# Global attention with its maxima in pairs of banks, its scores in single banks, its values two fifths at a time and the result's last two operations half a unit later

## The chip, the cores and the metric

One core of a Trainium2 chip runs the kernel. The metric is device time in microseconds (us) of one execution: 1538.0 us is the median of three (1535.93 to 1540.02). The engines are TensorE (PE, matrix products, with PEld for its weight loads), VectorE (DVE), ScalarE (ACT), GpSimd (POOL) and SyncE (SP), which issues the DMA transfers. "KB each" and shapes are those of the profile; everything is float32 unless a row says otherwise.

## The reference

Two layers (DEPTH) of a block over 1024 latent tokens and 256 context tokens, width 1024. One input projection feeds three groups of heads: A is global attention (8 heads of 64, 2 key heads, over all 1280 tokens), B a pooling mixer, C neighbourhood attention. Each result is multiplied by its own gate, all are joined and projected back:

```
aq, ak, av, ag, bz, bg, nq, nk, nv, ng = jnp.split(h @ w_in[l], SPLIT_POINTS, axis=-1)
...
def dense_attn(q, k, v):
    s = jnp.einsum("bqkgd,bskd->bkgqs", q, k).astype(jnp.float32)
    p = jax.nn.softmax(s, axis=-1).astype(v.dtype)
    o = jnp.einsum("bkgqs,bskd->bqkgd", p, v)
...
y = jnp.concatenate([a_out * silu(ag), b_out * silu(bg), n_out * silu(ng)], axis=-1) @ w_out[l]
x = x + gate[:, None] * y
```

## The kernel before, in words

Each layer runs in stages: the projections, the neighbourhood attention, the global attention, the output projection. The change is about the third stage and its seams with the second and fourth.

**The units of global attention.** There are 8 in a layer (`ga_unit`), each for 512 queries and a pair of heads of one key head. Scores are computed transposed: keys on the partitions, queries along the row. The 1280 keys are ten tiles of 128; two tiles make a fifth (`kp` 0 to 4). `scores(hi, kp)` does 4 matmuls for head `hi`, fifth `kp` (two tiles, each a product with `k1` and one with `k2`; the second also subtracts the softmax's shift, which lies in a row of `q2`) into a pair of banks, and ACT takes the exponential of all 1024 columns (L1032) into a tile `gp`. POOL adds the tiles of one head up (L1037 the first two, L1040 the next), DVE adds the last (L1040 too) and folds the halves (L1042). `values` multiplies a fifth with the value rows into the accumulator bank `ps_c`, one fifth behind the scores; the last copies the bank out (L1053, `gosb`).

**The maxima ("shifts").** The shift of the softmax is the exact row maximum, so the scores are computed once more with the queries on the partitions: per head 8 matmuls of 512 keys and 2 steps with 2 x 256 keys, each step in one single bank, each followed by a DVE reduction (L1004, L1009). These 20 steps of unit n, and a 21st that turns the result into a row (`shift_rows`, L1017, L1019, two small DMAs), are done ahead: a list `shifts` is worked off in between, 29 steps ahead of the scores. The first 29 are done in the last 10 units of the neighbourhood attention of layer 0 (the last 7 in layer 1), 3 per unit.

**The finish** of unit n comes within unit n+1, at `kp` 2: column sums (L1058, `ones` times the accumulators), a gate's DMA (L1060), logarithm and exponential for the reciprocal (ACT, L1062, L1063) with one correction step (DVE, L1065, L1066), gate times result (POOL, L1067), the product of both (DVE, L1068), and `store_u`, which splits it into a high part (ACT, L815) and a low part (DVE, L816). For the last unit it comes behind the first loads of the output projection's weights. Those are split the same way by `split_w` (ACT L287 high, DVE L288 low), three buffers `woraw`, one weight tile per k.

**What sets the order.** PE's instructions run in the order in which the code issues them (L97, `manual_schedule`). The orders of ACT, DVE, POOL and SP are made by the framework's scheduler; each engine then works its list strictly in order. PSUM has 8 banks: three single ones in rotation (`ps_b`, taken by `ps_one`), one accumulator (`ps_c`), and two pairs (`ps_w`, taken by `ps_pair`). The tiles `gp` and the accumulators `gacc` share a ring of seven buffers (tag "prob"); keys of both attentions share six buffers (`kst`).

**Neighbourhood attention** has 28 units in layer 0 (eight of them for the context's queries) and 16 in layer 1. `early(i, fn)` puts a load ahead of unit i: the queries of the first two global units at the twelfth unit from the end, the keys (`gk(0)`, three transfers) in both layers later. A unit waits on its own gate (L834), which goes through POOL (L869) before PE's transposes (L882).

Of the kernel before, what the change touches and what calls it, by code (L numbers as in the profile page):

```python
# [74 lines left out]
def hybrid_block_kernel(  # L75
# [298 lines left out]
    for l in range(DEPTH):  # L374
# [600 lines left out]
        def ga_unit(cc, g, pr):  # L975
# [16 lines left out]
            def shift(i):  # L992

                hi, j = divmod(i, 10)
                if i == 0:
# [4 lines left out]
                S = ps_one("ps_m")  # L1000
                if j < 8:
                    qt, half = divmod(j, 2)
                    PE.matmul(S, q1[:, qt * P:(qt + 1) * P], k1[:, half * 512:(half + 1) * 512], start=True, stop=True)  # L1003
                    DVE.reduce_max(out=mx[:, qt, half:half + 1], in_=S, axis=AX.X)  # L1004
                    return
                q0 = 2 * (j - 8)
                for i in range(2):
                    PE.matmul(S[:, i * 256:(i + 1) * 256], q1[:, (q0 + i) * P:(q0 + i + 1) * P], k1[:, SEQ:NT], start=True, stop=True)
                DVE.reduce_max(out=mx[:, q0:q0 + 2, 2], in_=S.rearrange("p (a b) -> p a b", a=2), axis=AX.X)  # L1009
                if hi and j == 9:  # L1010
                    st.nn = small.tile([P, 8], F32, tag="gnn", name="gnn")
                    DVE.tensor_reduce(out=st.nn, in_=st.mx.rearrange("p h q k -> p (h q) k"), op=ALU.max, axis=AX.X, negate=True)
# [11 lines left out]
            def scores(hi, kp):  # L1024
                k1, k2 = gk(g)
                S = ps_pair("ps_st").rearrange("p (a b) -> p a b", a=2)
                for i in range(2):
# [1 line left out]
                    PE.matmul(S[:, i, :], k1[:, kc], st.q1[hi], start=True, stop=False)  # L1029
                    PE.matmul(S[:, i, :], k2[:, kc], st.q2[hi], start=False, stop=True)  # L1030
# [1 line left out]
                ACT.activation(out=p, in_=S, func=AF.Exp)  # L1032
# [303 lines left out]
```

## Time and profile before

| | |
|---|---|
| median of three runs | 1538.0 us (1535.93 to 1540.02) |
| profiled execution | 1539.72 us, span 1537.9, clock 0.996 |
| busy PE, PEld, DVE, ACT, POOL | 1474.2, 1072.8, 860.2, 637.6, 513.1 us |
| a middle unit of global attention | 27.1 us, PE busy 25.85 |
| units 0, 6, 7 of layer 0 | 23.2, 26.7, 31.8 us |
| values, L1049 | x640, 165.0 us, mean 609 ns |
| maxima, L1004, DVE | x256, 171.7 us, mean 685 ns |
| exponentials, L1032, ACT | x160, 162.4 us, mean 1022 ns |
| adds, L1040, POOL | x64, 161.4 us, mean 2548 ns |

PE's row says "busy" from a matmul's start to its modelled end, and neighbours overlap; the distance of two starts shows what one really costs. In a row of waits stand the total, how often, and the longest; in a window's row its length, then busy time of PE, PEld, DVE, ACT and POOL, PE's clock, the share of the DMA engines and GB/s.

### The profile page before, as it was taken

To read this page: it belongs to the slowest core of one execution; us is meant where nothing else is said; L and a number is where in the kernel's file an instruction comes from. 1 tells how busy PE (TensorE), PEld (TensorE's weight loads), DVE (VectorE), ACT (ScalarE), POOL (GpSimd) and SP (SyncE) were. 2 spreads that over 40 slices of the span, in tenths; PEclk is the share of its full clock that TensorE was granted. 3 is DMA by queue.
4 is the path that set the end of the run, shared out by engine and by line. 5 is a ranking of instruction groups with operands and counts; after the bars stand their busy time and mean duration, and the time that the engine had idled before them with its cause. 6 is when DMAs were issued, how large, how long until landed. Compare 5 with 4: busy or idle time off the path is not lost.

```text
span 1537.9 us, 22259 instructions
## 1 busy us (share of the span) xinstructions
PE 1474.2 (96%) x8001; PEld 1072.8 (70%) x8001; DVE 860.2 (56%) x1666; ACT 637.6 (41%) x1220; POOL 513.1 (33%) x630
## 2 busy tenths in 40 slices
PE   5999999999999999998999999999998999999999
PEld 3787777788888555553788888878787854544577
DVE  3645234552678678875533543464358868786522
ACT  4543132333676444444312452332466544444400
POOL 0232336000134556565001233460013265565300
PEclk9999999999999999999999999999999999999999
DMA  9436455537745200101413222243697301001331
GB/s 317 140 97 219 133 158 162 165 107 192 178 113 159 73 27 25 39 8 55 168 58 109 76 93 91 85 142 82 155 227 172 89 21 42 21 24 39 133 121 55
DMA packets 153039, 167.91 MB, mean 109 GB/s; under 512 B 35384, under 2 KB 112032, under 8 KB 152864
## 3 DMA queue, kind: packets, MB, share of 16 engines
q1 hardware_dynamic: 152928, 166.48, 37.0%
q8 instruction: 63, 1.03, 0.3%
q14 instruction: 48, 0.39, 0.1%
HBM read 126.45 MB, written 40.86 MB: 109 GB/s over the span
## 4 chain that ended last, share of the span: by engine, by line
PE 80%; DVE 8%; ACT 4%; DMA 3%; issue 3%; SPq 1%; POOL 0%; DVEq 0%; POOLq 0%; ACTq 0%
PE ps_w L418 8%; PE ps_w L419 8%; PE ps_w L420 8%; PE ps_c L1049 8%; PE ps_w L1204 4%; PE ps_w L1207 4%; PE ps_w L1205 4%; PE ps_w L1029 4%; PE ps_b L1003 4%; PE ps_w L1030 3%; PE ps_c L894 3%; PE ps_b L882 2%; PE ps_w L426 2%; PE ps_w L428 2%; PE ps_w L427 2%
## 5 line engine op out<-in xcount | busy, mean ns | idle before, releaser
L1032 ACT ACTIVATE gp<-ps_w 128x1024 f32<-128x1024 f32 x160 | 162.4, 1022 | 190.9 <-PE ps_w L1030 155.3
L418 PE MATMUL ps_w<-wh,hh 128*128 128x512 f32 (+1 forms) x624 | 235.7, 378 | 2.2 <-ACT wh L287 2.2
L419 PE MATMUL ps_w<-wl,hh 128*128 128x512 f32 (+1 forms) x624 | 229.0, 367 | 1.0 <-DVE wl L288 1.0
L420 PE MATMUL ps_w<-wh,hl 128*128 128x512 f32 (+1 forms) x624 | 228.4, 366 | 0.0
L1004 DVE TENSOR_REDUCE gmx<-ps_b 128x1 f32<-128x512 f32 x256 | 171.7, 685 | 73.2 <-PE ps_b L1003 69.0
L1049 PE MATMUL ps_c<-gp,av 128*64 128x512 f32 x640 | 165.0, 609 | 10.3 <-ACT gp L1032 10.3
L1040 POOL TENSOR_TENSOR gacc<-gacc,gp 128x1024 f32<-128x1024 f32 x64 | 161.4, 2548 | 25.8 <-ACT gp L1032 25.5
L418 PEld LDWEIGHTS ps_w<-wh,hh 128*128 128x128 f32 x624 | 118.4, 190 | 27.8 <-issue 4.0
L419 PEld LDWEIGHTS ps_w<-wl,hh 128*128 128x128 f32 x624 | 117.8, 189 | 21.3 <-DVE wl L288 2.2
L420 PEld LDWEIGHTS ps_w<-wh,hl 128*128 128x128 f32 x624 | 117.6, 188 | 21.3
L1030 PE MATMUL ps_w<-gq,kst 128*128 128x512 f32 x320 | 126.7, 396 | 0.0
L1204 PE MATMUL ps_w<-woh,hh 128*128 128x512 f32 x272 | 109.5, 403 | 0.0
L1205 PE MATMUL ps_w<-wol,hh 128*128 128x512 f32 x272 | 107.4, 395 | 0.0
L639 DVE TENSOR_REDUCE qss<-sq 128x8 f32<-128x512 f32 (+2 forms) x58 | 31.1, 537 | 135.7 <-ACT sq L637 135.7
L1049 PEld LDWEIGHTS ps_c<-gp,av 128*64 128x64 f32 x640 | 42.5, 136 | 87.3 <-issue 65.2
L1037 POOL TENSOR_TENSOR gacc<-gp 128x1024 f32<-128x1024 f32 x32 | 75.8, 2369 | 50.0 <-ACT gp L1032 50.0
L288 DVE TENSOR_TENSOR wl<-wraw,wh 128x512 fp32r<-128x512 f32 (+1 forms) x96 | 66.3, 707 | 38.8 <-ACT wh L287 37.4
L1207 PE MATMUL ps_w<-woh,hl 128*128 128x512 f32 x272 | 85.6, 395 | 0.0
L426 PE MATMUL ps_w<-hh,wh 128*128 128x512 f32 (+1 forms) x208 | 81.6, 392 | 2.4 <-ACT wh L287 2.4
L866 ACT ACTIVATE prob<-ps_w,m 128x768 f32<-128x768 f32 (+2 forms) x88 | 72.7, 826 | 19.4 <-DVE m L853 7.4
L428 PE MATMUL ps_w<-hh,wl 128*128 128x512 f32 (+1 forms) x208 | 79.6, 382 | 0.0
L427 PE MATMUL ps_w<-hl,wh 128*128 128x512 f32 (+1 forms) x208 | 79.2, 381 | 0.0
(225 smaller groups left out, 2916.2 us busy)
## 6 DMA issues: line engine op xcount, KB each, us to landing
wmod<-in_w_mod_dram SPq DMA_DIRECT2D x48, 512.0 KB
wraw<-in_w_in_dram SPq DMA_DIRECT2D x64, 256.0 KB
gq<-qad SPq DMA_DIRECT2D x64, 128.0 KB
woraw<-in_w_out_dram SPq DMA_DIRECT2D x14, 512.0 KB
wraw<-in_w_in_dram SPq DMA_DIRECT2D x48, 128.0 KB
kst<-knd SPq DMA_DIRECT2D x16, 320.0 KB
qad<-qkhi SPq DMA_DIRECT2D x18, 256.0 KB
qad<-qklo SPq DMA_DIRECT2D x18, 256.0 KB
```

The costliest lines, as they stand in the source:

```text
L418: PE.matmul(ps[:, :n], a, wh[:, off:off + n], start=(k == 0), stop=False)
L419: PE.matmul(ps[:, :n], a, wl[:, off:off + n], start=False, stop=False)
L420: PE.matmul(ps[:, :n], b, wh[:, off:off + n], start=False, stop=(k == KT - 1))
L426: PE.matmul(ps[:, :n], wh[:, fs], hh[:, k, ts_], start=(k == 0), stop=False)
L1004: DVE.reduce_max(out=mx[:, qt, half:half + 1], in_=S, axis=AX.X)
L1030: PE.matmul(S[:, i, :], k2[:, kc], st.q2[hi], start=False, stop=True)
L1032: ACT.activation(out=p, in_=S, func=AF.Exp)
L1040: eng.tensor_tensor(out=st.acc[hi], in0=st.acc[hi], in1=pf, op=ALU.add)
L1049: PE.matmul(st.o[hi * 64:(hi + 1) * 64, :], av[:, kt, g * 64:(g + 1) * 64], st.p[hi, kp][:, i, :], start=(kt == 0), stop=(kt == NTT - 1))
L1204: PE.matmul(ps[:, i2, :], a, oh[:, cs], start=(k == 0), stop=False)
L1205: PE.matmul(ps[:, i2, :], a, ol[:, cs], start=False, stop=False)
L1207: PE.matmul(ps[:, i2, :], b, oh[:, i2 * 512:(i2 + 1) * 512], start=False, stop=(k == KT - 1))
```

## The change

- **Scores** take a single bank per tile of keys, with an exponential of 512 columns each (now L1053), two per fifth.
- **Maxima** take a pair of banks: 5 steps per head (4 with 2 x 512 keys, L1028; one with 4 x 256, L1032), 11 steps per unit with the row step. Only the first three heads, done within the neighbourhood attention, keep the old way. 31 steps are now ahead, one per half of a unit, in the last 16 units of the neighbourhood attention: in layer 1 from its first unit. `gk(0)` and the first queries are loaded ahead of that, in layer 1 at unit 0.
- **Values** come in blocks of two fifths, at `kp` 2 and 4; the last fifth at `kp` 1 of the next unit, with the sums (now in a pair, L1079) and the finish right behind it.
- **The finish** leaves both last products to POOL (L1089, L1090). The high and low parts (L1094 ACT, L1095 DVE) are a function of their own, `finish2`, called at `kp` 4.
- **The accumulators** leave the ring: even units use memory of `nv`, odd ones two key buffers. In unit 7 the adds of head 0 are DVE's (L1061).

The core of the diff:

```diff
-GA_AHEAD = 8
+GA_AHEAD = 31
...
-                early(s0 + 4, lambda: gk(0))
+                pass
...
+            def shift2(hi, j):
+
+                if j == 0:
+                    (load2 if hi else shift_new)()
+                S = ps_pair("ps_m")
+                if j < 4:
+                    for half in range(2):
+                        shift_mm(hi, S, j, half * 512, half * 512, 512)
+                    DVE.reduce_max(out=st.mx[:, hi, j, 0:1], in_=S, axis=AX.X)
+                    return
+                for qt in range(4):
+                    shift_mm(hi, S, qt, qt * 256, SEQ, 256)
+                DVE.reduce_max(out=st.mx[:, hi, :, 1], in_=S.rearrange("p (a b) -> p a b", a=4), axis=AX.X)
+                shift_head(hi, 2)
...
-                S = ps_pair("ps_st").rearrange("p (a b) -> p a b", a=2)
+                p = ap_.tile([P, 2, 512], F32, name="gp", tag="prob", bufs=PB)
                 for i in range(2):
+                    S = ps_one("ps_st")
...
-                ACT.activation(out=p, in_=S, func=AF.Exp)
+                    ACT.activation(out=p[:, i, :], in_=S, func=AF.Exp)
...
-                    st.acc[hi] = ap_.tile([P, 1024], F32, name="gacc", tag="prob", bufs=PB)
+                    st.acc[hi] = accs[n % 2][hi]
...
-                    eng = DVE if kp == 4 else POOL
+                    eng = DVE if kp == 4 or (n == 7 and hi == 0) else POOL
...
-                POOL.tensor_tensor(out=gt, in0=gt, in1=st.osb, op=ALU.mult)
-                DVE.scalar_tensor_tensor(out=t1, in0=t1, scalar=-1.0, in1=gt, op0=ALU.mult, op1=ALU.mult)
-                store_u(f, cc * 512, 512, t1)
+                POOL.tensor_tensor(out=st.gt, in0=st.gt, in1=st.osb, op=ALU.mult)
+                POOL.tensor_tensor(out=st.gt, in0=st.gt, in1=t1, op=ALU.mult)
+
+            def finish2():
+                hi, lo = hh[:, f, cs], hl[:, f, cs]
+                ACT.activation(out=hi, in_=st.gt, func=AF.Identity, scale=-1.0)
+                DVE.scalar_tensor_tensor(out=lo, in0=st.gt, scalar=-1.0, in1=hi.bitcast(F32), op0=ALU.mult, op1=ALU.subtract)
...
+                way, k = (0, 10) if i + hi < 2 and i < 2 else (6, 5)
+                own += [lambda u=u, way=way, hi=hi, j=j: u[way](hi, j) for j in range(k)]
...
+        n_shifts = min(len(units), (GA_AHEAD + 1) // 2)
         for i in range(2):
-            early(len(units) - 12, gunits[i][4])
+            early(len(units) - n_shifts - 1, gunits[i][4])
+        early(len(units) - n_shifts, lambda: gk(0))
...
             for kp in range(5):
...
                 scores(0, kp)
                 shift_step(1)
-                if lagv:
-                    lagv(0)
-                    lagv(1)
-                shift_step(2 if kp == 4 else 1)
+
+                if kp == 1 and pv:
+                    pv[2](4, 0)
+                    pv[2](4, 1)
+                    pv[7]()
+                    pv[3]()
+                elif kp in (2, 4):
+                    for j in range(4):
+                        values(kp - 2 + j // 2, j % 2)
+                if kp == 4 and pv:
+                    pv[8]()
                 scores(1, kp)
-                shift_step(2)
-                if kp == 2 and pv:
-                    pv[3]()
+                shift_step(2 if kp == 0 else 1)
...
         gunits[-1][3]()
+        gunits[-1][8]()
```

(`pv[2]`, `[7]`, `[3]`, `[8]` are values, sums, finish and finish2 of the unit before.) What the scheduler makes of it is shown at three places.

*ACT in the middle of a middle unit of layer 0.* Before: the exponentials of (0,2) and (1,2), then the reciprocal of the unit before, (0,3), (1,3), the high part L815, the row of maxima, (0,4).

```order
L1032 ACTIVATE gp_6476<-ps_w0_3845 128x1024
L1032 ACTIVATE gp_6491<-ps_w1_3846 128x1024
L1062 ACTIVATE gr0_6506<-ps_b1_70 128x512
L1063 ACTIVATE gr0_6506<-gr0_6506 128x512
L1032 ACTIVATE gp_6520<-ps_w0_3845 128x1024
L1032 ACTIVATE gp_6542<-ps_w1_3846 128x1024
L815 ACTIVATE hh_95<-gt1_6509 128x512
L1019 ACTIVATE gmr_6546<-ps_b1_70 8x128
L1032 ACTIVATE gp_6556<-ps_w0_3845 128x1024
```

After, on ACT, from the second half of (0,1) (`gp_6277`) through (1,1) (`gp_6306`) and (0,2) (`gp_6320`) to (1,2) (`gp_6341`):

```order
L1053 ACTIVATE gp_6277<-ps_b2_71 128x512
L1074 ACTIVATE gosb_6292<-ps_c_72 128x512
L1085 ACTIVATE gr0_6297<-ps_w0_3845 128x512
L1053 ACTIVATE gp_6306<-ps_b0_69 128x512
L1086 ACTIVATE gr0_6297<-gr0_6297 128x512
L1053 ACTIVATE gp_6306<-ps_b1_70 128x512
L1053 ACTIVATE gp_6320<-ps_b2_71 128x512
L1053 ACTIVATE gp_6320<-ps_b0_69 128x512
L1094 ACTIVATE hh_95<-ggate_6296 128x512
L1053 ACTIVATE gp_6341<-ps_b1_70 128x512
L1053 ACTIVATE gp_6341<-ps_b2_71 128x512
```

The high part of the unit before now stands ahead of (1,2), where it stood behind (1,3). Its input comes from POOL, whose list in the same unit is, after the change:

```order
L1058 TENSOR_TENSOR gacc_5755<-gp_6248,gp_6277 128x1024
L1089 TENSOR_TENSOR ggate_6296<-ggate_6296,gosb_6292 128x512
L1058 TENSOR_TENSOR gacc_5756<-gp_6264,gp_6306 128x1024
L1061 TENSOR_TENSOR gacc_5755<-gacc_5755,gp_6320 128x1024
L1090 TENSOR_TENSOR ggate_6296<-ggate_6296,gt1_6298 128x512
L1061 TENSOR_TENSOR gacc_5756<-gacc_5756,gp_6341 128x1024
L1061 TENSOR_TENSOR gacc_5755<-gacc_5755,gp_6352 128x1024
L1061 TENSOR_TENSOR gacc_5756<-gacc_5756,gp_6365 128x1024
```

Before, POOL had the six adds in a row and one product (L1067) behind them; now the product L1090 stands fifth, behind the add of (0,2).

*ACT at the end of layer 0.* Before:

```order
L1053 ACTIVATE gosb_7007<-ps_c_72 128x512
L1062 ACTIVATE gr0_7041<-ps_b0_69 128x512
L287 ACTIVATE woh1_7018<-woraw0_7014 128x1024
L1063 ACTIVATE gr0_7041<-gr0_7041 128x512
L287 ACTIVATE woh2_7020<-woraw1_7015 128x1024
L287 ACTIVATE woh3_7022<-woraw2_7030 128x1024
L815 ACTIVATE hh_95<-gt1_7044 128x512
L287 ACTIVATE woh4_7024<-woraw0_7014 128x1024
```

After:

```order
L1074 ACTIVATE gosb_7016<-ps_c_72 128x512
L1085 ACTIVATE gr0_7049<-ps_w0_3845 128x512
L1086 ACTIVATE gr0_7049<-gr0_7049 128x512
L1094 ACTIVATE hh_95<-ggate_7048 128x512
L287 ACTIVATE woh1_7029<-woraw0_7025 128x1024
L287 ACTIVATE woh2_7031<-woraw1_7026 128x1024
```

All of the finish now stands ahead of the first split of the projection's weights; on DVE the low part (L1095) likewise stands ahead of the first L288.

*SP at the seam of projections and neighbourhood attention in layer 1.* Before, two loads for queries of the global attention (`qad`), then keys (`knd`) and gates (`ngd`) of the neighbourhood attention:

```order
L372 DMA hh_95<-qad_77 64x512 x2
L730 DMA agd_81<-gate_10520 128x512
L372 DMA hl_96<-qad_77 64x512
L793 DMA hh_95<-knd_80 64x1280 x2
L834 DMA ngate_10590<-ngd_83 128x128
```

After:

```order
L372 DMA hh_95<-qad_77 64x512 x2
L730 DMA agd_81<-gate_10529 128x512
L372 DMA hl_96<-qad_77 64x512 x2
L372 DMA hh_95<-qad_77 64x512 x2
L372 DMA hl_96<-qad_77 64x512 x2
L755 DMA kst_10607<-kad_78 64x1280 x2
L761 DMA kst_10610<-kad_78 64x1280
L834 DMA ngate_10614<-ngd_83 128x128
```

All queries of the first two global units and the keys of the first key head now stand ahead of the first gate; PE's first maxima stand right behind its last gate projection.

More of the change, by code (lines that the diff above doesn't have):

```diff
@@ L1002, in shift @@
                     qt, half = divmod(j, 2)
[L1003 to L1004 removed]
+                    shift_mm(hi, S, qt, 0, half * 512, 512)
+                    DVE.reduce_max(out=st.mx[:, hi, qt, half:half + 1], in_=S, axis=AX.X)
                     return
@@ L1007, in shift @@
                 for i in range(2):
[L1008 to L1012, printed above, removed]
+                    shift_mm(hi, S, q0 + i, i * 256, SEQ, 256)
+                DVE.reduce_max(out=st.mx[:, hi, q0:q0 + 2, 2], in_=S.rearrange("p (a b) -> p a b", a=2), axis=AX.X)
+                if j == 9:
+                    shift_head(hi, 3)
+            def shift2(hi, j):
+                if j == 0:
+                    (load2 if hi else shift_new)()
+                S = ps_pair("ps_m")
[8 more added lines that the diff above has]
+                shift_head(hi, 2)
             def shift_rows():
@@ L1053, in values, with sums @@
                     ACT.activation(out=st.osb, in_=st.o, func=AF.Copy)
+            def sums():
+                st.s = ps_pair("ps_gs")[:, 0:512]
+                for hi in range(2):
+                    PE.matmul(st.s[hi * 64:(hi + 1) * 64, :], ones, st.acc[hi][:, 0:512], start=True, stop=True)
             def finish():
-                s_ps = ps_one("ps_gs")
-                for hi in range(2):
-                    PE.matmul(s_ps[hi * 64:(hi + 1) * 64, :], ones, st.acc[hi][:, 0:512], start=True, stop=True)
@@ L1069, in finish @@
-                store_u(f, cc * 512, 512, t1)
-            return shift, scores, values, finish, load, shift_rows
-        gunits = [ga_unit(cc, g, pr) for cc in range(2) for g in range(2) for pr in range(2)]
+                POOL.tensor_tensor(out=st.gt, in0=st.gt, in1=st.osb, op=ALU.mult)
[4 more added lines that the diff above has]
+                DVE.scalar_tensor_tensor(out=lo, in0=st.gt, scalar=-1.0, in1=hi.bitcast(F32), op0=ALU.mult, op1=ALU.subtract)
@@ L1075, in hybrid_block_kernel @@
+            return shift, scores, values, finish, load, shift_rows, shift2, sums, finish2
+        gunits = [ga_unit(4 * cc + 2 * g + pr, cc, g, pr) for cc in range(2) for g in range(2) for pr in range(2)]
         shifts = []
         for i, u in enumerate(gunits):
-            own = [lambda u=u, j=j: u[0](j) for j in range(20)]
+            own = []
+            for hi in range(2):
+                way, k = (0, 10) if i + hi < 2 and i < 2 else (6, 5)
+                own += [lambda u=u, way=way, hi=hi, j=j: u[way](hi, j) for j in range(k)]
@@ L1136, in hybrid_block_kernel @@
         nu = len(gunits)
+        nvf = nv.rearrange("p t c -> p (t c)")
+        accs = [[nvf[:, 0:1024], nvf[:, 1024:2048]],
+                [ak_.tile([P, NT], F32, name="gacc", tag="kst", bufs=6)[:, 0:1024] for _ in range(2)]]
         for i in range(nu):
-            _, scores, values, finish, _, _ = gunits[i]
+            _, scores, values, finish = gunits[i][:4]
             pv = gunits[i - 1] if i else None
```

52 lines of the change are left out of this document (21 added, 31 removed).

## The prediction

> **What bounds the kernel now.** The page comes first: the engines' shares, then the chain that ended last.
>
> ```profile
> PE 1474.2 (96%) x8001; PEld 1072.8 (70%) x8001; DVE 860.2 (56%) x1666; ACT 637.6 (41%) x1220; POOL 513.1 (33%) x630
> PE 80%; DVE 8%; ACT 4%; DMA 3%; issue 3%; SPq 1%; POOL 0%; DVEq 0%; POOLq 0%; ACTq 0%
> ```
>
> TensorE (PE) is the bound on average. The change lies in the global attention of both layers, so the windows of its units come second; in layer 0 they are unit 0, one of the five middle units, unit 6 and unit 7, then the projection behind them. The first number behind the window is its length, the second PE's busy time.
>
> ```profile
> 513.00:536.20 23.20, 23.02 (x105) 13.33 (x101) 14.38 (x21) 10.12 (x11) 15.34 (x9) 1.00 0.04 12
> 588.20:615.30 27.10, 25.85 (x111) 13.75 (x110) 21.51 (x31) 12.64 (x15) 16.32 (x7) 1.00 0.10 30
> 671.70:698.40 26.70, 24.82 (x102) 12.58 (x101) 19.24 (x24) 11.50 (x14) 15.89 (x7) 1.00 0.14 50
> 698.40:730.20 31.80, 28.43 (x97) 12.31 (x95) 14.98 (x12) 13.58 (x16) 16.19 (x8) 0.95 0.08 25
> 731.00:760.00 29.00, 29.00 (x126) 23.12 (x125) 17.23 (x21) 10.93 (x15) 0.13 (x1) 1.00 0.52 181
> ```
>
> A middle unit takes 27.1 us and PE lacks 1.25 us of it; unit 7 takes 31.8, though it computes no maxima. Third, PE's waits in the middle units (561 to 696), then in unit 7 (698 to 731):
>
> ```profile
> PE ps_b L1003 <- DVE gmx L1004: 6.2, 5, 1.2
> PE ps_c L1049 <- ACT gp L1032: 3.3, 2, 3.1
> ```
>
> So each middle unit loses 1.2 us to the maxima's single banks, at its start. Elsewhere order and count of PE's instructions set the time. There is little idle time to win: a gain has to come from PE's own work, and each new wait costs in full.
>
> **The change part by part.** *PE's own work.* What do turns between scores and values cost? PE's timeline:
>
> ```profile
> 712.97 0.40 PE L1030 MATMUL ps_w<-gq,kst 128*128 128x512 f32 x1
> 713.30 1.94 PE L1049 MATMUL ps_c<-gp,av 128*64 128x512 f32 x8
> 715.17 0.50 PE L1029 MATMUL ps_w<-hl,kst 128*128 128x512 f32 x1
> 715.51 0.39 PE L1030 MATMUL ps_w<-gq,kst 128*128 128x512 f32 x1
> 715.74 0.40 PE L1029 MATMUL ps_w<-hl,kst 128*128 128x512 f32 x1
> 711.16 1.08 PE L1058 MATMUL ps_b<-gacc,ones 128*64 128x512 f32 x4
> ```
>
> Matmuls start 0.23 apart (715.51, 715.74). A block of one fifth's values holds 1.87 (713.30 to 715.17), the step into it is 0.10 longer than 0.23 and the step out 0.11: 2.08. The sums take 1.0. A middle unit of before is then 60 x 0.23 (40 scores, maxima equal to 20 wide ones) + 5 x 2.08 + 1.0 + 0.15 for the shift rows = 25.4; with the wait of 1.2 it is 26.6 of 27.1 measured. After, one block of 2.08 and two of 3.95 (2 x 1.87 + 0.21): 13.8 + 10.0 + 1.0 + 0.15 = 24.9, plus the 0.3 to 0.5 that the count misses: 25.2 to 25.4 without waits. I take 25.2, that is 1.9 less than now.
>
> *ScalarE (ACT) behind GpSimd (POOL).* The order puts line 1094 of each unit between exp(0,2) and exp(1,2) of the next; it waits for line 1090, the fifth POOL operation of that unit. Durations, from the groups of the middle units:
>
> ```profile
> L1032 ACT ACTIVATE gp<-ps_w 128x1024 f32<-128x1024 f32 x50 | 51.0, 1021 | 58.4 <-PE ps_w L1030 45.7 <-POOL gacc L1037 12.7
> L1053 ACT ACTIVATE gosb<-ps_c 128x512 f32<-128x512 f32 x5 | 3.0, 598 | 5.3 <-PE ps_c L1049 5.3
> L815 ACT ACTIVATE hh<-gt 128x512 fp32r<-128x512 f32 x5 | 3.2, 630 | 7.4 <-DVE gt L1068 7.4
> L1040 POOL TENSOR_TENSOR gacc<-gacc,gp 128x1024 f32<-128x1024 f32 x20 | 51.1, 2586 | 8.0 <-ACT gp L1032 8.0
> L1037 POOL TENSOR_TENSOR gacc<-gp 128x1024 f32<-128x1024 f32 x10 | 23.7, 2366 | 15.1 <-ACT gp L1032 15.1
> L1067 POOL TENSOR_TENSOR ggate<-ggate,gosb 128x512 f32<-128x512 f32 x5 | 6.5, 1292 | 33.2 <-ACT gosb L1053 33.2
> ```
>
> Count from a middle unit's start. PE has done 18 matmuls, the old fifth and the sums by 7.6 (18 x 0.23 + 2.08 + 1.0 = 7.2, and gaps). ACT's queue there: L1085 to 8.3, first half of exp(1,1) to 8.9, L1086 to 9.5, second half to 10.1. POOL: the sum for (1,1) to 12.5, that for (0,2) to 15.05, L1090 (as L1067) to 16.35. L1094 ends at 17.0 and the first half of exp(1,2) at 17.6. PE, with three single banks, runs to scores (0,3) at 15.4 (7.6 + 12 x 0.23 + 3.95 + 4 x 0.23 + 0.15) and there wants that very bank: it waits 2.2. With POOL's shortest adds (2.35 each) it is 1.9; were POOL to start a full add earlier, nothing. I take 2.0. Two half-width exps cost ACT 2 x 0.60 for 1.02: 1.8 per unit more, hidden, since ACT is busy for 12.64 of 27.1.
>
> *Maxima in pairs.* A reduction of 1024 isn't in the trace; 256 and 512 columns are:
>
> ```profile
> L850 DVE TENSOR_REDUCE m<-ps_w 128x1 f32<-128x256 f32 x88 | 37.1, 422 | 24.9 <-PE ps_w L847 23.7
> L1004 DVE TENSOR_REDUCE gmx<-ps_b 128x1 f32<-128x512 f32 x76 | 50.9, 685 | 24.1 <-PE ps_b L1003 22.8
> L1040 DVE TENSOR_TENSOR gacc<-gacc,gp 128x1024 f32<-128x1024 f32 x10 | 12.1, 1211 | 0.0
> L1042 DVE TENSOR_TENSOR gacc<-gacc 128x512 f32<-128x512 f32 x10 | 6.8, 677 | 0.0
> ```
>
> 0.263 more for 256 columns gives an estimate of 1.21 for 1024; ten of them are 12.1 against 20 x 0.685 = 13.7, so VectorE (DVE) gains 1.6 per unit, off the path. On the path is the start of a unit. From the last maxima of one unit to the third pair of the next, DVE has one reduction, the add for (1,4), a small head (0.2), one more reduction: 1.21 + 1.21 + 0.2 + 1.21 = 3.8, while PE needs 12 x 0.23 = 2.8 to come back to the pair. That wait is 1.0, against 1.2 measured today; at its best 0, at its worst 1.5, when the fold (0.68) comes ahead of a second pair. I take 0.6.
>
> A middle unit then takes 25.2 + 2.0 + 0.6 = 27.8, or **+0.7 x 5 = +3.5 per layer**.
>
> *Units 0, 6 and 7.* Unit 0 has no finish: two blocks fewer turns and no wait, -0.8. Unit 6: PE's 1.9 less and the new wait against it, -0.3. Unit 7 is today held by the ring of seven buffers, by POOL and by L815, which stands ahead of two exps and waits for DVE:
>
> ```profile
> 719.80 0.63 ACT L815 ACTIVATE hh<-gt 128x512 fp32r<-128x512 f32 x1 [5.15 <-DVE gt L1068]
> 721.39 2.81 PE L1049 MATMUL ps_c<-gp,av 128*64 128x512 f32 x6 [3.08 <-ACT gp L1032]
> ```
>
> After, the accumulators are out of the ring and half of the adds are DVE's, so L1090 stands behind two POOL adds, not three. PE's work is 40 x 0.23 + 2.08 + 7.9 + 1.0, and 3.1 for the tail: 23.3. With 2.5 for waits 25.8: -6. Per layer these are -7.1.
>
> *The end of a layer.* Today the first weights of the projection are split beside the last finish:
>
> ```profile
> 730.27 0.50 PE L1204 MATMUL ps_w<-woh,hh 128*128 128x512 f32 x1
> 730.87 1.05 ACT L287 ACTIVATE woh<-woraw 128x1024 fp32r<-128x1024 f32 x1
> 731.95 1.23 DVE L288 TENSOR_TENSOR wol<-woraw,woh 128x1024 fp32r<-128x1024 f32 x1 [2.74 <-ACT woh L287]
> 735.62 0.69 DVE L1068 SCALAR_TENSOR_TENSOR gt<-gt,ggate 128x512 f32<-128x512 f32 x1
> ```
>
> After, L1085, L1086 and L1094 precede every L287 on ACT, and L1095 every L288 on DVE. From the sums' end: 0.1 + 0.60 + 0.63 + 0.69 (L1087) + 0.69 (L1088, as L1068 here) + 1.29 + 0.63 + 1.05 = 5.7 until the second weights' high half, 1.23 more for the low one: 6.9. PE has 12 matmuls with the first weights and one with the second: 13 x 0.23 = 3.0. **+4 per layer**; at least 2.9 (the high half alone), and 0 only if ACT didn't keep the order.
>
> *The maxima's earlier start and its transfers.* In layer 1 the keys and queries (three keys' loads and the queries') move to unit 0 of the neighbourhood attention, where the queue is full (1125 to 1140):
>
> ```profile
> DMA packets 1927, 3.46 MB, mean 231 GB/s; under 512 B 286, under 2 KB 790, under 8 KB 1926
> hh<-knd SPq DMA_DIRECT2D x3, 320.0 KB
> hh<-qad SPq DMA_DIRECT2D x2, 128.0 KB
> 1165.00:1170.00 5.00, 2.38 (x33) 1.85 (x32) 3.47 (x8) 3.71 (x8) 2.08 (x10) 1.00 0.12 36
> 1135.00:1226.00 91.00, 83.89 (x843) 74.18 (x840) 74.29 (x188) 59.41 (x120) 28.10 (x75) 1.00 0.62 148
> 487.00:512.00 25.00, 22.10 (x166) 15.69 (x165) 22.01 (x62) 15.09 (x49) 11.96 (x36) 1.00 0.49 140
> ```
>
> About 1.6 MB earlier is 7 us of the queue. PE's first maxima stand right behind the last gate projection; they and the gates behind them in the queue can come 4 to 7 us late. Against that stand 7.1 idle us of 1135 to 1226 that sparser maxima can fill, as 2.9 of 487 to 512 in layer 0. I take +2 in layer 1 (-3 to +8) and -1 in layer 0.
>
> **Sum.** 2 x (3.5 - 7.1 + 4) + 2 - 1 = +1.8 us on the profiled execution's 1539.7, which lies 1.7 over the median; on the median 1538.0 it is **1539.8 us**.
>
> **The rivals.** *(a) The ACT wait is hidden.* If L1090 comes a full add earlier, a middle unit takes 25.8, 2.0 less than in my sum: 10 x -2.0 = -20, **1520 us**. For it: POOL is idle 10.8 of 27.1 in a middle unit, and 1.2 of PE's present wait is gone anyway; against it: the adds' input chain has been counted step by step and POOL takes them in order.
>
> *(b) Slower: DVE locked out at the unit's end.* The add for (0,4) on DVE now falls beside POOL's add for (1,3). What such a pair does, the trace has:
>
> ```profile
> 690.49 2.85 POOL L1040 TENSOR_TENSOR gacc<-gacc,gp 128x1024 f32<-128x1024 f32 x1
> 691.19 2.69 DVE L1068 SCALAR_TENSOR_TENSOR gt<-gt,ggate 128x512 f32<-128x512 f32 x1
> ```
>
> The DVE operation takes 2.69 and ends 0.54 behind POOL's, where it takes 0.69 alone. The Trainium skill ("SBUF — State Buffer", section "Who interferes with whom") has a rule for that: a VectorE instruction with two inputs in SBUF and a GpSimd one that reads SBUF lock each other out for the whole instruction. These rows agree with it, 0.54 apart. In the middle unit the add for (0,4) may start at 23.2 with POOL's (1,3), and ends at 26.3 instead of 24.4; every reduction behind it waits, and the start of the next unit costs 1.5 instead of 0.6. It decides if more than two reductions queue behind it. 10 x 0.9 = +9: **1549 us**.
>
> *(c) The transfers of layer 1 cost 8, not 2:* 1546 us. For it: 2.6 of the 5 us at 1165 to 1170 are lost already; against it: the share is 0.62 over the stretch.
>
> *(d) Unit 7 doesn't get shorter,* since moved adds only put DVE in POOL's place: +6 per layer, 1552 us.
>
> **How the numbers follow.** My forecast has 0.45 (own range 1533 to 1547, from the bounds of the two waits), (a) 0.32, (b) 0.13, (c) and (d) 0.05 each. Over 0.3% (4.6 us, about what a measurement of this kernel tells from no change) faster: (a) and 0.10 of the forecast: 0.42. Within: 0.22, from the forecast. Slower: its other 0.13 and the rest: 0.36. (a) with POOL's bounds reaches to 1514, (b) with a full wait in the ACT queue to 1550; beyond both lies about 0.2.
>
> **What would show it.** Right: in a middle unit a PE wait of about 2 us for ACT at scores (0,3), with ACT itself waiting for POOL L1090; a unit of 27 to 28.5; unit 7 near 26; a gap of about 4 us on PE some 3 us into each projection, released by ACT L287 or DVE L288. Wrong: middle units under 26.5, a projection without a gap, or a loss at 1134 to 1175 of over 8 us.

## The result, and the profile after

The changed kernel takes 1545.65 us (median of 8 runs, 1542.98 to 1546.76), the kernel before 1537.74 (8 runs, 1532.88 to 1540.02): a ratio of 1.0051 with an interval of 1.0039 to 1.0062. It is 7.9 us slower; the forecast was 1.8 slower.

The page's shares and the chain that ended last, of the kernel after:

```profile
PE 1466.4 (95%) x8001; PEld 1072.3 (69%) x8001; DVE 848.9 (55%) x1540; ACT 644.0 (42%) x1380; POOL 520.3 (34%) x642
PE 74%; DVE 8%; ACT 5%; issue 5%; POOL 4%; DMA 3%; SPq 1%; POOLq 0%; ACTq 0%; DVEq 0%
```

PE is busy for 7.8 us less, as the change meant: 1474.2 became 1466.4. But the chain runs over PE for 74% instead of 80% of a longer span, and POOL, which had none of it, has 4%. Work went, and waits came. PE's waits over the whole span:

```profile
PE ps_w L1001 <- DVE gmx L1028: 10.8, 12, 1.0
PE ps_w L1001 <- DVE gt L1087: 9.9, 10, 1.0
PE ps_b L1001 <- DMA kst<-kad: 5.7, 1, 5.7
PE ps_b L1051 <- ACT gp L1053: 5.0, 5, 1.5
PE ps_w L1237 <- ACT woh L287: 4.2, 2, 2.1
PE ps_w L1238 <- DVE wol L288: 1.4, 2, 0.8
```

The first two rows are about 0.9 and 1.0 us each, once in a unit; the third is the start of layer 1's maxima. The fourth, the wait that the prediction looked for in the middle units, lies in units 6 and 7 (0.9 and 1.5 in each layer; the fifth is 0.2). The last two are the ends of the two layers, 2.1 and 0.7 each.

The stages, from the start of PE's first matmul in one to that in the next, in the two profiled executions (us):

| stage | before | after | difference |
|---|---|---|---|
| a middle unit of global attention | 27.13 | 28.15 | +1.0, ten times |
| unit 0 | 22.84, 22.78 | 22.32, 22.40 | -0.5, -0.4 |
| unit 6 | 26.70, 26.70 | 26.34, 26.29 | -0.4, -0.4 |
| unit 7 | 31.86, 31.83 | 25.81, 25.81 | -6.0, -6.0 |
| projection, first to last matmul | 117.37, 78.70 | 123.04, 85.44 | +5.7, +6.7 |
| neighbourhood attention | 121.32, 99.98 | 120.64, 103.35 | -0.7, +3.4 |

These add up to +11.6, while the two spans differ by 6.9. The rest lies in stretches that the change doesn't touch: the start until the first neighbourhood scores was 2.2 shorter in the profile after, that from layer 0's last projection matmul to layer 1's neighbourhood attention 2.6 (279.1 against 276.5; 276.3 in a second profile of the kernel before). In both, the profile before has 3.4 us of half clock (PE's granted clock is 0.50 from 152.3 to 155.6 and from 1091.0 to 1094.3) that the profile after lacks. That second profile shows too how far single profiles carry: its unit 6 takes 28.4 and 28.3, not 26.7, its layer 1 neighbourhood attention 100.8, all else in global attention is within 0.2. Unit 6 has the same wait of 1.9 us for an exponential in both profiles; behind it the clock is 0.57 in the second (692 to 696) and 1.00 in the first (694 to 698).

One middle unit after, 28.2 long, then unit 7, and the start of layer 0's projection in three pieces; the last three columns are PE's granted clock, DMA share and GB/s:

```profile
589.00:617.20 28.20, 25.93 (x111) 13.75 (x111) 20.66 (x20) 13.02 (x26) 17.07 (x8) 1.00 0.10 29
699.90:725.70 25.80, 24.25 (x97) 10.52 (x95) 17.66 (x13) 13.78 (x27) 15.08 (x8) 1.00 0.26 89
725.70:731.60 5.90, 3.35 (x13) 2.11 (x12) 2.09 (x4) 2.85 (x5) 1.65 (x2) 1.00 0.04 15
731.00:734.00 3.00, 1.63 (x4) 1.15 (x5) 2.75 (x4) 2.45 (x3) 0.00 (x0) 0.86 0.04 4
734.00:737.00 3.00, 3.00 (x9) 2.33 (x8) 1.08 (x1) 0.00 (x0) 0.00 (x0) 0.57 0.78 264
```

From 734 to 737 PE is "busy" for the whole 3.00 us and yet starts 9 matmuls, where it starts 15 in the 3 us behind: the granted clock is 0.57 on average, 0.5 until 736.6 and 1.0 from there. The gap costs twice, once as a wait and once as half speed behind it. At the end of layer 1 the half clock lasts twice as long (1450.0 to 1456.8), behind the same gap:

```profile
1453.00:1456.00 3.00, 3.00 (x9) 2.32 (x8) 0.94 (x2) 1.06 (x1) 0.00 (x0) 0.50 0.94 246
```

Inside a middle unit (start 589.04): the timeline of PE, of DVE, and of POOL and ACT.

```profile
592.93 0.73 PE L1001 MATMUL ps_w<-kst,hl 128*128 128x512 f32 x2 [0.95 <-DVE gmx L1028]
597.09 1.03 PE L1079 MATMUL ps_w<-nv,ones 128*64 128x512 f32 x4
601.64 0.73 PE L1001 MATMUL ps_w<-kst,hh 128*128 128x512 f32 x2 [0.99 <-DVE gt L1087]
607.62 0.40 PE L1052 MATMUL ps_b<-gq,kst 128*128 128x512 f32 x1
608.14 0.50 PE L1051 MATMUL ps_b<-hh,kst 128*128 128x512 f32 x1
```

```profile
589.32 1.22 DVE L1032 TENSOR_REDUCE gmx<-ps_w 128x4 f32<-128x1024 f32 x1
590.46 1.22 DVE L1061 TENSOR_TENSOR nv<-nv,gp 128x1024 f32<-128x1024 f32 x1
591.66 1.21 DVE L1028 TENSOR_REDUCE gmx<-ps_w 128x1 f32<-128x1024 f32 x1
600.91 0.68 DVE L1087 TENSOR_TENSOR gt<-ps_w,gr 128x512 f32<-128x512 f32 x1
613.49 3.36 DVE L1061 TENSOR_TENSOR gacc<-gacc,gp 128x1024 f32<-128x1024 f32 x1
```

```profile
605.66 1.28 POOL L1090 TENSOR_TENSOR ggate<-ggate,gt 128x512 f32<-128x512 f32 x1
608.72 7.05 POOL L1061 TENSOR_TENSOR gacc<-gacc,gp 128x1024 f32<-128x1024 f32 x3 [1.78 <-ACT gp L1053]
606.98 0.63 ACT L1094 ACTIVATE hh<-ggate 128x512 fp32r<-128x512 f32 x1 [5.52 <-POOL ggate L1090]
```

The wait at 592.93 is the queue that the prediction added up: reduction 589.32, add for (1,4) 590.46, reduction 591.66. The next pair comes 0.24 late as well: those maxima start 0.47 behind the matmul before them (594.19 to 594.66), not 0.23. The wait at 601.64 it didn't have: the sums now lie in a pair, line 1087 is the last to read it, and DVE gets to that only at 600.91. ACT does stand for 5.5 us for POOL's last product, which ends 8.9 us behind the sums' end (598.05), as forecast (8.75). But PE is held there for only 0.3 us (608.14 instead of 607.85). Together: 25.6 of PE's own work (measured below) and waits of 0.95, 0.24, 1.0 and 0.3 make 28.1.

### The profile page after: what moved, and what is told of

It reads as the page before. It is cut to its first block, busy times and chain, and to the rows that moved or that the text cites. A ratio compares the mean times of both kernels' runs of the same rounds, so it can differ in the third digit from the quotient of the medians.

```text
span 1544.8 us, 22288 instructions
## 1 busy us (share of the span) xinstructions
PE 1466.4 (95%) x8001; PEld 1072.3 (69%) x8001; DVE 848.9 (55%) x1540; ACT 644.0 (42%) x1380; POOL 520.3 (34%) x642
## 4 chain that ended last, share of the span: by engine, by line
PE 74%; DVE 8%; ACT 5%; issue 5%; POOL 4%; DMA 3%; SPq 1%; POOLq 0%; ACTq 0%; DVEq 0%
PE ps_w L418 8%; PE ps_w L419 8%; PE ps_w L420 8%; PE ps_c L1070 5%; PE ps_w L1238 4%; PE ps_w L1237 4%; PE ps_w L1240 4%; PE ps_c L894 4%; PE ps_b L882 3%; ACT gp L1053 3%; PE ps_b L1051 3%; PE ps_w L426 2%; PE ps_w L428 2%; PE ps_w L427 2%; PE ps_w L846 2%
## 5 line engine op out<-in xcount | busy, mean ns | idle before, releaser
L1053 ACT ACTIVATE gp<-ps_b 128x512 f32<-128x512 f32 x320 | 170.5, 598 | 122.2 <-PE ps_b L1052 120.4
L1070 PE MATMUL ps_c<-gp,av 128*64 128x512 f32 x640 | 148.5, 600 | 0.0
L1028 DVE TENSOR_REDUCE gmx<-ps_w 128x1 f32<-128x1024 f32 x104 | 124.4, 1219 | 30.0 <-PE ps_w L1001 30.0
L1052 PE MATMUL ps_b<-gq,kst 128*128 128x512 f32 x320 | 126.2, 394 | 0.0
L288 DVE TENSOR_TENSOR wl<-wraw,wh 128x512 fp32r<-128x512 f32 (+1 forms) x96 | 66.7, 711 | 38.2 <-ACT wh L287 36.6
L866 ACT ACTIVATE prob<-ps_w,m 128x768 f32<-128x768 f32 (+2 forms) x88 | 72.6, 825 | 25.2 <-DVE m L853 12.0
L1061 POOL TENSOR_TENSOR nv<-nv,gp 128x1024 f32<-128x1024 f32 x32 | 78.0, 2461 | 12.7 <-ACT gp L1053 12.7
L637 ACT ACTIVATE sq<-ps_w 128x512 f32<-128x512 f32 (+2 forms) x58 | 27.9, 481 | 122.9 <-PE ps_w L420 122.9
```

The costliest lines, as they stand in the source:

```text
L1028: DVE.reduce_max(out=st.mx[:, hi, j, 0:1], in_=S, axis=AX.X)
L1052: PE.matmul(S, k2[:, kc], st.q2[hi], start=False, stop=True)
L1053: ACT.activation(out=p[:, i, :], in_=S, func=AF.Exp)
L1070: PE.matmul(st.o[hi * 64:(hi + 1) * 64, :], av[:, kt, g * 64:(g + 1) * 64], st.p[hi, kp][:, i, :], start=(kt == 0), stop=(kt == NTT - 1))
```

## The experiments

All are the changed kernel with edits. `tc.issue_after(x)` queues what stands under it behind instruction x on x's engine, with no wait added. Ratios are to the kernel before, which was run again beside each group of experiments; its medians lie between 1536.04 and 1538.72, so a difference of some 2 us between two groups may be no more than that.

**The layer's end (e1_end).** The splits of two projection weights go ahead of the last high and low part:

```diff
         for k in range(1, 3):
-            load_wo(k)
+            sa, sd = load_wo(k)
         gunits[-1][3]()
-        gunits[-1][8]()
+        with tc.issue_after(sa.ins), tc.issue_after(sd.ins):
+            gunits[-1][8]()
```

(`split_w` and `load_wo` return their two instructions.)

> The changed kernel with one edit: at the end of a layer the splits of the second and third projection weights (ACT and DVE) are issued ahead of the last unit's high and low part. My theory: the projection's gap of 2.1 + 0.8 us, and with it the slow stretch of matmuls that follows it (starts 0.43 us apart instead of 0.23 for some 4 us), come from that order alone. Expected: from the first to the last matmul of the projection 117 instead of 123 us in layer 0 and 79 instead of 85 in layer 1, together 11 to 12 us off the total, 1534. Rival: the slow stretch has another cause (the weights' transfers, which run at that time); then only the waits go, 6 us in all, 1540.

Measured: 1534.22 us, 0.9979 (0.9962 to 0.9995), 11.4 less than the change; the projections take 118.3 and 79.7 (4.7 and 5.7 less). PE's waits from 721 to 760, and the window in which the change had half clock, now at 1.00:

```profile
PE ps_w L1239 <- DVE gt L1088: 0.5, 1, 0.5
```

```profile
731.00:737.00 6.00, 6.00 (x27) 4.84 (x26) 2.91 (x3) 3.19 (x3) 0.00 (x0) 1.00 0.90 317
```

The first row is all that is left of waits, the clock in the second is full. The weights' transfers run here too (share 0.90), so they are not what slows matmuls: with the gap goes the half speed. In the ten profiles that have the gap, half clock follows it at 19 of the 20 layer ends; at the 20th (layer 1 of e4_add) the clock stays 1.00 and the projection is 1.5 us shorter. A good 10 of the change's 12 us at the projections are the order of ACT and DVE there, and with this one edit the changed kernel is a little under the one before.

**Layer 1's transfers, later (e2_l1).** Loads and maxima from the eleventh unit from the end on:

```diff
-        n_shifts = min(len(units), (GA_AHEAD + 1) // 2)
+        n_shifts = 11 if last else min(len(units), (GA_AHEAD + 1) // 2)
...
-                    shift_step(1, n_least)
+                    shift_step(2 if last and hi else 1, n_least)
```

> The changed kernel with one edit: in layer 1 the maxima start at the eleventh unit from the end of the neighbourhood attention, three per unit, instead of at the first unit, and the loads of keys and queries with them. My theory: the wait of 5.7 us for the keys and the slow stretch behind it (about 2 us) go, and nothing comes in their place: the neighbourhood attention of layer 1 takes 96 instead of 103.4 us, the total 1538. Rival: the transfers are short of room wherever they stand, and gates come late instead: at least 101 us, 1543 or more.

Measured: 1547.13 us, 1.0054 (1.0034 to 1.0075); the neighbourhood attention of layer 1 takes 106.7, not 96. It is as slow as the rival said, but what comes late is the keys again, more than a gate:

```profile
PE ps_b L1001 <- DMA kst<-kad: 3.8, 1, 3.8
PE ps_b L1001 <- ACT probt L887: 5.6, 9, 1.3
```

The keys are waited for at the sixth unit as well, and three maxima in a unit wait for single banks.

**Same transfers, later use (e7_use).** Loads as in the change, first maxima from the fourth unit on:

```diff
-                if n >= nun - n_shifts:
-                    shift_step(1, n_least)
+                if n >= (3 if last else nun - n_shifts):
+                    shift_step(2 if last and hi and n < 8 else 1, n_least)
```

> The changed kernel with one edit: in layer 1 the loads of keys and queries stay where they are, at the first unit of the neighbourhood attention, but the first maxima are computed from the fourth unit on (three per unit in five units, then two). Theory: what costs is that PE, in order, stands at the first maxima until the keys land, not the transfers' place in the queue; without that wait of 5.7 us and the slow stretch behind it the neighbourhood attention takes 96 to 98 instead of 103.4 us and the total is 1538 to 1540. Rival: the gates, which lie behind these loads in the queue, come late instead, and it stays over 101 us, 1543 or more.

Measured: 1548.35 us, 1.0082 (1.0064 to 1.01); 104.3 us. The rival again: no wait for the keys, but one of 5.3 us for a gate that lies behind them in the queue:

```profile
PE ps_b L882 <- POOL rg L869: 7.8, 6, 5.3
```

**Layer 1 as before (e11_l1old).** Keys loaded at the first maxima, in the last seven units, three steps each:

```diff
-            early(len(units) - n_shifts - 1, gunits[i][4])
-        early(len(units) - n_shifts, lambda: gk(0))
+            early(len(units) - (12 if last else n_shifts + 1), gunits[i][4])
+        if not last:
+            early(len(units) - n_shifts, lambda: gk(0))
...
-                if n >= nun - n_shifts:
-                    shift_step(1, n_least)
+                if n >= nun - (7 if last else n_shifts):
+                    shift_step(2 if last and hi else 1, n_least)
```

> The changed kernel with one edit: layer 1 of the neighbourhood attention as in the kernel before (keys loaded at the first maxima, in the last seven units, three steps a unit). Theory: the layout of before costs as much elsewhere (the steps that are left over, three maxima in a unit), so the neighbourhood attention keeps 102 to 104 us and the total 1544 to 1547. Rival: the early transfers are what the 3.4 us of layer 1 are; it takes 100 us, the total 1542.

Measured: 1544.14 us, 1.0047 (1.003 to 1.0065); 102.0 us. Between the two, nearer to the theory. The wait for the keys of 5.7 us is real, but most of it is paid for by units with two maxima instead of three: they take 4.9 to 5.6 us, against 5.7 to 6.8 with three. What the start of layer 1's maxima costs in the end is 1.5 us or less, about the spread of a median.

**Line 1087 first (e3_ref).** On DVE the last reader of the sums' pair goes ahead of the reduction before it:

```diff
-                    pv[3]()
+                    st_dve = pv[3]()
...
                 scores(1, kp)
-                shift_step(2 if kp == 0 else 1)
+                if kp == 1 and pv:
+                    with tc.issue_after(st_dve.ins):
+                        shift_step(1)
+                else:
+                    shift_step(2 if kp == 0 else 1)
```

(`finish` returns the instruction of line 1087.)

> The changed kernel with one edit: on DVE the product of sums and reciprocal (line 1087), which is the last to read the sums' pair of banks, goes ahead of the reduction that stood before it. PE's wait of 1.0 us for that pair in each unit goes. Theory 1, the waits replace each other: POOL's chain to the last product starts at the sums and is not shortened, so the wait of PE for the exponential behind the high part grows from 0.3 to 1.2 and a middle unit stays within 0.2 us of 28.15; total 1543 to 1546. Theory 2, the waits add up: a middle unit takes 27.2 and the total is 1535 to 1537.

Measured: 1547.76 us, 1.0055 (1.0034 to 1.0076). PE's waits in the middle units of layer 0:

```profile
PE ps_b L1051 <- ACT gp L1053: 5.0, 5, 1.0
PE ps_w L1001 <- DVE gmx L1028: 4.6, 5, 0.9
```

Theory 1: the wait for line 1087 is gone, that for the exponential is now 1.0 in each unit, and the middle units keep 28.15. Sums, reciprocal, adds and product are one chain through ACT and POOL; what PE saves beside it, it waits at its end. (The total isn't lower but 2 higher: in unit 6 of both layers the row of maxima now waits 3.0 for DVE, where it was 1.1. The unit takes 27.1 and 28.7 instead of 26.3; in layer 1 half clock follows that wait, 0.53 from 1406.4 to 1410.0, in layer 0 it doesn't, 1.00 from 688.0 to 691.4.)

**The high part later too (e5_refact).** The edit above, and ACT's line 1094 behind the exponentials of (1,3):

```diff
-                    pv[8]()
-                scores(1, kp)
+                    with tc.issue_after(last_exp.ins):
+                        pv[8]()
+                last_exp = scores(1, kp)
```

> The changed kernel with two edits: line 1087 ahead of the reduction as in the run before, and the high part of the result (ACT) behind the exponentials of (1,3) instead of ahead of those of (1,2). Theory: the two waits replaced each other because the exponential of (1,2) hung on POOL's chain; freed of it, PE gains both, 1.3 us, a middle unit takes 26.9 and the total is 1533. Rival: a third queue takes over (DVE with its locked add, or POOL's adds for the next sums) and a middle unit stays over 27.7, the total over 1541.

Measured: 1549.33 us, 1.0089 (1.0071 to 1.0108). Unit 1 takes 26.8, but the other middle units 27.9 to 29.15: the rival. The wait at a unit's start is now 1.6, and in the three units over 29 half clock follows it. Unit 6 takes 28.1, with the wait of 3.0 of the run before. PE's waits in the middle units of layer 0, and DVE:

```profile
PE ps_w L1001 <- DVE gmx L1028: 7.2, 5, 1.6
```

```profile
584.38 3.38 DVE L1061 TENSOR_TENSOR nv<-nv,gp 128x1024 f32<-128x1024 f32 x1
587.68 1.21 DVE L1028 TENSOR_REDUCE gmx<-ps_w 128x1 f32<-128x1024 f32 x1
```

The scheduler now set the add for (0,4) ahead of a reduction. It runs locked beside POOL's add, 3.4 instead of 1.2 us, and the reduction behind it is what PE wants.

**That add held back (e9_order).** The edits above (line 1087 not in unit 6, where it had cost the 3.0), and the add and fold of head 0 emitted behind the maxima of that half unit:

```diff
                 scores(0, kp)
                 shift_step(1)
+                if kp == 4:
+                    gunits[i][9](0)
...
+                    a = DVE.tensor_tensor(out=st.acc[0], in0=st.acc[0], in1=st.p[0, 4].rearrange("p a b -> p (a b)"), op=ALU.add)
+                    tc.keep_in_program_order(a)
```

> The edits of e5_refact (line 1087 first except in unit 6, the high part behind the exponentials of (1,3)), and on DVE the last add of head 0 held behind the reduction of that half unit. Theory: the middle units of e5_refact lost what they had won because the scheduler set this add, which runs locked beside POOL's add for 3.4 us, ahead of a reduction for which PE waits; behind it the lock falls where no one waits. A middle unit takes 26.9, the total is 1533. Rival: the lock only moves on; a middle unit stays over 27.7, the total over 1541.

Measured: 1527.58 us, 0.9935 (0.9917 to 0.9954). All ten middle units take 26.8 to 26.95, as expected; units 6 and 7, 25.3 and 24.4, gain too. The same DVE instructions, and PE's waits in the middle units of layer 0:

```profile
609.09 1.21 DVE L1028 TENSOR_REDUCE gmx<-ps_w 128x1 f32<-128x1024 f32 x1
610.23 2.25 DVE L1068 TENSOR_TENSOR gacc<-gacc,gp 128x1024 f32<-128x1024 f32 x1
```

```profile
PE ps_w L1001 <- DVE gmx L1028: 5.7, 6, 1.0
```

Only the wait at the units' starts is left (the sixth is unit 6's). The lock still takes place, but where no one waits for DVE. The three orders weren't tried one by one: the two runs before show that the first alone and the first two don't do, not what the third would do alone.

**An add moved to POOL (e4_add).** The last add of head 1 in units 0 to 6, its fold on DVE at `kp` 1 of the next unit:

```diff
-                    eng = DVE if kp == 4 or (n == 7 and hi == 0) else POOL
+                    eng = DVE if kp == 4 and (hi == 0 or n == 7) or (n == 7 and hi == 0) else POOL
...
                 if kp == 1 and pv:
+                    tc.keep_in_program_order(pv[9](1))
                     pv[2](4, 0)
```

(`pv[9]` is the fold of the unit before, now a function of its own.)

> The changed kernel with one edit: the last add of head 1 in units 0 to 6 goes from DVE to POOL, and its fold on DVE behind the first reductions of the next unit. Theory: PE's wait at a unit's start (0.95 and 0.24 us) is DVE's queue of reduction, add and reduction; without the add it goes, and a middle unit takes 27.0; twelve units make 14 us, total 1532. Rival: the wait is that of the locked add of head 0 (3.4 us beside POOL's add), which stays: a middle unit keeps 28.1 and the total is 1545; or POOL, with one add more, comes late for the sums, and the unit gets longer.

Measured: 1553.98 us, 1.0098 (1.0069 to 1.0127); a middle unit takes 28.46. The wait at the start is gone, as the theory had it, but the fold comes late for the sums, locked beside POOL's next add; unit 7 grew to 28.15, where the sums wait 1.3 for the same fold. POOL, DVE and PE:

```profile
598.42 2.35 POOL L1058 TENSOR_TENSOR gacc<-gp 128x1024 f32<-128x1024 f32 x1 [2.41 <-ACT gp L1053]
599.49 1.82 DVE L1066 TENSOR_TENSOR nv<-nv 128x512 f32<-128x512 f32 x1
601.37 1.07 PE L1082 MATMUL ps_w<-nv,ones 128*64 128x512 f32 x2 [0.55 <-DVE nv L1066]
```

**All three together (e6_mid).** The edits of e5_refact, the add of units 0 to 5 on POOL, and the fold between two reductions:

```diff
+                elif kp == 0:
+                    shift_step(1)
+                    if 0 < i < 7:
+                        folded = tc.keep_in_program_order(pv[9](1))
+                        with tc.issue_after(folded.ins):
+                            shift_step(1)
```

> The edits of the run before, and the last add of head 1 in units 0 to 5 on POOL, with its fold on DVE between the second and third reduction of the next unit, where POOL reads nothing. Theory: the wait at a unit's start (1.2 us) goes as well and isn't given back at the sums, since the fold is no longer late; a middle unit takes 25.7 to 25.9, which is PE's own work, and the total is 1521 to 1524. Rival: the adds on POOL or the fold are late again; a middle unit takes 26.9 or more, the total 1533 or more.

Measured: 1557.11 us, 1.0138 (1.0122 to 1.0154). Unit 1 is what was expected; it stands behind unit 0, which has no finish, and DVE comes to it in time. The next ones take 26.6 to 30.3, so the rival came true:

```profile
532.60:558.20 25.60, 25.30 (x111) 13.80 (x110) 18.93 (x18) 13.06 (x26) 19.92 (x9) 1.00 0.11 31
558.20:588.50 30.30, 27.25 (x111) 14.36 (x110) 22.23 (x19) 13.14 (x26) 19.96 (x9) 0.94 0.09 27
```

```profile
554.47 3.38 DVE L1061 TENSOR_TENSOR gacc<-gacc,gp 128x1024 f32<-128x1024 f32 x1
557.77 1.21 DVE L1028 TENSOR_REDUCE gmx<-ps_w 128x1 f32<-128x1024 f32 x1
558.91 2.78 DVE L1067 TENSOR_TENSOR gacc<-gacc 128x512 f32<-128x512 f32 x1
558.74 2.40 POOL L1061 TENSOR_TENSOR gacc<-gacc,gp 128x1024 f32<-128x1024 f32 x1 [1.97 <-ACT gp L1053]
```

```profile
PE ps_w L1001 <- DVE gmx L1032: 8.6, 4, 2.2
```

25.6 is PE's own work in such a unit. Around the start of the next one the add and the fold of head 0 both run locked, the more POOL adds, the more DVE's adds wait, and PE waits 2.2 for the reduction behind them (last row: the middle units of layer 0). Where half clock follows that wait the unit takes 30.2 or 30.3, elsewhere 28.7; one unit that is spared the wait takes 26.6.

**Unit 7's adds (e8_u7).** Head 0 back on POOL:

```diff
-                    eng = DVE if kp == 4 or (n == 7 and hi == 0) else POOL
+                    eng = DVE if kp == 4 else POOL
```

> The changed kernel with one edit: in unit 7 the adds of head 0 are POOL's again. Theory: two things made unit 7 shorter, the accumulators out of the ring and the adds on DVE, and the adds are worth a part: with one add more ahead of the last product the high part comes 2.4 us later and PE waits for it; unit 7 takes 28 to 28.5 instead of 25.8, the total is 1550. Rival: the ring alone did it; unit 7 stays under 26.5, the total at 1546.

Measured: 1550.39 us, 1.009 (1.0074 to 1.0106); unit 7 takes 29.1 and 28.4. The high part of unit 6 in the change, then in this run, and PE's waits in this run's unit 7 of layer 0:

```profile
713.38 0.63 ACT L1094 ACTIVATE hh<-ggate 128x512 fp32r<-128x512 f32 x1 [4.32 <-POOL ggate L1090]
```

```profile
715.81 0.63 ACT L1094 ACTIVATE hh<-ggate 128x512 fp32r<-128x512 f32 x1 [5.51 <-POOL ggate L1090]
```

```profile
PE ps_b L1051 <- ACT gp L1053: 2.7, 1, 2.7
PE ps_w L1079 <- DVE gacc L1063: 1.7, 1, 1.7
```

The size is the theory's, the way only in part. Unit 7 starts at 699.9 in the change and at 701.1 here, so the high part comes 1.2 us later within it, not 2.4, and PE waits 2.7 for the exponential behind it, not 1.5. In layer 0 the rest is a wait that the theory didn't have, 1.7 of the last sums for the fold of the accumulator; in layer 1 that one is missing, but half clock follows the first (1435.9 to 1439.3). So of the 6 us of unit 7 about 3 are the adds on DVE and 3 the rest (ring, fewer turns), which wasn't taken apart.

**What is best of it (e10_best).** The edits of e9_order, e1_end and e11_l1old:

> The edits of e9_order and of e1_end, and the maxima of layer 1 as in the kernel before (keys and first queries later, three steps a unit in the last seven units). If the parts add up, by the theory: 1533 less 11.5 for the ends of the layers and 2 to 3 for layer 1, that is 1519; by the rival for the middle units 1530. Either would be under the kernel before.

Measured: 1516.11 us, 0.9861 (0.9842 to 0.988), 22.6 less than the kernel before. A middle unit:

```profile
580.00:607.00 27.00, 25.73 (x111) 13.84 (x111) 20.09 (x19) 13.08 (x27) 17.60 (x9) 1.00 0.10 31
```

The middle units take 26.9, units 6 and 7 25.3 and 24.4, the projections 118.3 and 79.7. The time of e9_order less the 11.4 of e1_end is 1516.2: that is all of it, so layer 1's layout was worth nothing here (103.1 us either way).

A second profile of the kernel before was taken for the spread:

> The kernel before once more, for a second profile: how far the neighbourhood attention of layer 1 (100.0 us in the first) differs from run to run. If it varies by 2 us or more, the 3.4 us that layer 1 lost are within that.

Its layer 1 took 100.8 (one execution, 1537.49 us), within 1 us of the first. With the changed layout seven profiles show 102.6 to 103.6 and one 100.7, with that of before 102.0 and 103.1. So layer 1 did lose 2 to 3 us, and the transfers' place explains at most half of it. Part of the rest is the clock. Behind the same wait of 2.6 us for a gate it is full in the kernel before (first row) and half in e11_l1old (second row), where PE starts 32 matmuls instead of 43:

```profile
1168.00:1171.50 3.50, 3.50 (x43) 3.21 (x44) 2.22 (x5) 0.89 (x3) 1.79 (x7) 1.00 0.45 133
1165.50:1169.00 3.50, 3.50 (x32) 3.17 (x29) 1.33 (x3) 0.34 (x1) 1.32 (x6) 0.51 0.78 190
```

The profile with 100.7 (e8_u7) has one stretch of half clock there, of 3.4 us, the change two, of 6.8 and 3.4. What is left beside that stays open.

## Why the prediction was right or wrong

The time lies in the range, on the slower side of the forecast, which had given "slower" a chance of 0.36. That it does is in part luck: the steps were to add up to +1.8, and in the profiles the stages come to +11.6, which alone would have made some 1550, over the range. Of the difference 4.4 are the layers' ends, 3.2 the middle units, 1.7 the neighbourhood attention. Step by step:

- **PE's own work, 25.2 in a middle unit:** 25.6 measured where nothing waits (unit 1 of e6_mid). The count of turns was right to 0.4.
- **The ACT wait, 2.0:** the queues came out as worked out, the product 8.9 instead of 8.75 behind the sums; the price was mis-sized, 0.3. The step that failed is "PE, with three single banks, runs to scores (0,3) at 15.4 ... and there wants that very bank": the maxima of that half unit come in between, the first tile of (0,3) takes the third bank, and only the second wants the one that waits. And PE came 1.0 us later than counted, because of the wait that was missing; without it the ACT wait is 1.0 (e3_ref). It does stand in units 6 and 7, with 0.9 and 1.5.
- **A wait that was missing, 1.0:** sums in a pair take one of only two pairs from the maxima until line 1087 has read it. The same pair holds the projection's start for 0.5, which no step had either.
- **The start of a unit, 0.6 between 0 and 1.5:** the queue gave 1.0, and I took less for no reason in a row; measured 0.95, and 0.24 at the pair behind it.
- **A middle unit:** +0.7 forecast, +1.0 measured, from other parts than thought.
- **Units 0, 6 and 7:** -0.8, -0.3 and -6 forecast, -0.5, -0.4 and -6.0 measured. That unit 7 comes out to the tenth is luck: 23.3 of work and 2.5 of waits were forecast, and PE is busy for 24.25 and waits 1.5. Rival (d) fell: the adds on DVE are what it has to thank for half of it.
- **The layer's end, +4:** the waits were nearly right (2.1, 0.8 and 0.5 in layer 0, 3.4 against 3.9), but the size was 5.7 and 6.7. The sum counted the gap and not the half clock behind it, 3.4 us of it in layer 0 and 6.8 in layer 1. The kernel before has such a stretch in unit 7, behind its wait of 3.1 us (its windows, clock third from the end; the half clock, 722.3 to 725.7, fills a little over half of each):

```profile
721.00:724.00 3.00, 2.61 (x6) 0.56 (x6) 1.79 (x2) 1.25 (x2) 2.35 (x1) 0.72 0.00 0
724.00:727.00 3.00, 3.00 (x7) 1.35 (x6) 1.60 (x2) 0.87 (x1) 0.00 (x0) 0.71 0.00 0
```

  The Trainium skill ("TensorE: Matmul & The Clock Gate", "Part 1: The HAM clock gate") has PE at half rate after an idle window of about 3.4 us, until it was busy for as long. The traces agree on the rate (starts 0.43 apart instead of 0.23) and in layer 0 on the length (733.2 to 736.6), but the waits here were 2.1 and 0.8 with one matmul between, and half clock followed waits of 1.6 (e5_refact). By that rule the layer's end would have been forecast 1.7 us dearer (an estimate: half of the Trainium skill's 3.4), at 5.7, which is what layer 0 shows.
- **Layer 1's transfers, +2 (-3 to +8):** about +3 in the stage, of which the layout gives back 1.5 or less (e11_l1old). Layer 0's -1 was -0.7.
- **Rival (a),** the hidden ACT wait: it was nearly hidden, and the 20 us didn't come, since other waits stood in its place. **Rival (b),** the locked add: it takes 3.4 us in each unit, where 3.1 was said, but the reduction behind it started at 589.32, right behind its matmuls (the last two from 588.81); the start of a unit hangs on what follows. It decides as soon as anything else is freed (e5_refact, e6_mid).

## What to carry to other kernels

Where several engines' queues run in step, price a wait by the cycle it lies on: taking away one wait moved the same microsecond to the next queue, until three instructions had been moved. Compare the lists of all engines after a change, not only the one that was edited; what turned 1546 into 1516 here was the place of four kinds of instruction in their queues (line 1087, the high part, one add, the splits of the weights). And a gap on PE can cost twice: in these traces half clock followed 19 of the 20 gaps of 2.1 and up to 0.8 us at a layer's end, but 2 of the 6 waits of 3.0 in unit 6 (e3_ref, e5_refact, e6_mid) and 3 of the 10 of 1.6 in e5_refact. Each stretch of 3.4 us at half clock is worth up to 1.7 us. So look at a profile's clock before you explain a microsecond or two of it by its queues.
